# Norms finished in token layout and turned by plain transposes, instead of float32 matmuls with a diagonal matrix

## The chip, the cores and the metric

The kernel runs on one core of a Trainium2 chip, written in Bass with the Tile framework, which fixes the order of each engine's instructions before the run. The metric is the device time in microseconds of one execution; a kernel is timed in several runs, and the median counts. The engines are TensorE (PE), VectorE (DVE), ScalarE (ACT), GpSimd (POOL) and SyncE (SP, which issues the loads).

## What is computed

Two transformer blocks on S = 256 tokens with D = 1024 features, all in float32. The first has two layers, the second two more:

```python
def rms_norm(x, g):
    y = xf * lax.rsqrt(jnp.mean(xf * xf, axis=-1, keepdims=True) + EPS)
    return (y * g.astype(f32)).astype(x.dtype)
def layer_norm(x, g, b):
    mu = jnp.mean(xf, -1, keepdims=True)
    var = jnp.mean(jnp.square(xf - mu), -1, keepdims=True)
    return ((xf - mu) * lax.rsqrt(var + LN_EPS) * g + b).astype(x.dtype)

def even_layer(x, ...):  z = rms_norm(x, g_norm) @ w_in; ...; return x + y @ w_out   # two attentions
def odd_layer(x, ...):   z = rms_norm(x, g_norm) @ w_in; ...; return x + (y * silu(g)) @ w_out   # retention
def first_block(x, ...): return rms_norm(odd_layer(even_layer(x)), final_norm)

def second_block(x, ...):
    h = layer_norm(x, ln_in_g, ln_in_b)
    for l in range(DEPTH):               # DEPTH = 2
        m = hybrid_mixer(h, ...)
        h = layer_norm(ALPHA * h + m, ln1_g[l], ln1_b[l])
        f = swiglu(h, ...) if l % 2 == 0 else moe_swiglu(h, ...)   # dense, then 8 experts, top 2
        h = layer_norm(ALPHA * h + f, ln2_g[l], ln2_b[l])
    return h
```

## The kernel before

**Layout.** The activations x stay in SBUF as [128 tokens, 2 tiles, 1024 features]. Products with weights need them turned, features on partitions. So each norm writes `xT[0]` and `xT[1]`, [128 features, 8 chunks, 256 tokens]: two float32r parts (high and low) whose sum is the float32 value. The weights stream from HBM as raw float32 into `w_raw`, in units of 128 x 2048. ACT copies each into its high part `w_hi` (L56), DVE subtracts for the low part `w_lo` (L58). A float32 product is then three matmuls, hi x hi, hi x lo and lo x hi (`mm3`, L177 to L179).

**Order around a norm.** `out_units` computes the last matrix product ahead of a norm. Its last four weight units go tile by tile of the tokens: first all matmuls of tile 0 (48, with 512 columns, into two PSUM banks), then the 48 of tile 1. As soon as tile 0 is emitted, `done(0, acc[0])` emits its norm, then come the matmuls of tile 1; the scheduler places the instructions of both on each engine. The norm of tile 1 is kept in `self.late` and emitted by `finish`, after the next `token_units` has emitted the matmuls of tile 0 for its three units (24 each, 256 columns); those of tile 1 follow. Ahead of the experts it is the 16 small matmuls of the router that stand in place of the three units. Two tiles each for the norms at the start, behind the even layer (RMS norms), behind the odd layer, mixer 0, the feed-forward and mixer 1 (layer norms) make twelve tile norms. A last layer norm behind the experts goes to the output and is not turned.

**One norm of a tile.** On DVE: for a layer norm x * ALPHA + acc (L344) and the statistics (L345, L347), (x - mean) * g (L356), and the factor r = 1/sqrt(var) by Newton steps on 128x1 values (`rsqrt`, L286 to L296). Then `diagonal` (L372) makes a 128x128 matrix with r on its diagonal. `transpose` multiplies each 128x128 chunk of x by it on PE as a float32 matmul (L386; the trace shows each as two passes), which turns and scales at once. For a layer norm, the shift b is added in the same bank by a bfloat16 matmul first (L382), from a table of three-part shifts that the start loads and splits. From PSUM, ACT copies the high parts and DVE subtracts the low ones (L406; L394 and L398 where RMS scales are applied). x itself gets r * x + b only later (L364), in `rows_later` three units on, or in the experts spread over ACT and POOL.

Of the kernel before, what the change touches and what calls it, by code (L numbers as in the profile page):

```python
# [15 lines left out]
ALU = mybir.AluOpType  # L16
# [8 lines left out]
class Weights:  # L25
    """The weights in the order of their use: loaded and split into two float32r parts ahead of it."""
# [48 lines left out]
class Side:  # L75
    """Work in stages that goes between the weight units. A stage that yields "pre" has its next one before a unit."""
# [39 lines left out]
class Stack:  # L116
    def __init__(self, nc, tc, ctx, a, out, order, dbg=None):
# [11 lines left out]
        self.pend, self.late, self.update, self.todump = [], None, [], None  # L129
# [7 lines left out]
    def spare(self):  # L137
        """A buffer [128, 2, 1024] among those of the weights."""
        return self.wpools[0].tile([128, 2048], F32, name="w_raw")[:].rearrange("p (t d) -> p t d", t=2)

    def rows(self, *aps, queue=None):
        """One or two rows of 1024, on all partitions."""
        t = self.spare()
        for i, ap in enumerate(aps):
            if ap is None:
                continue
            (queue or self.nc.gpsimd).dma_start(t[:, i, :], bass.AP(tensor=ap.tensor, offset=ap.offset,  # L147
                                                                  ap=[[0, 128], [1, D]]))
        return [t[:, i, :] for i in range(len(aps))]

    def load_shifts(self):
        for g in range(2):
            for j in range(3):
                p = 64 * g + 8 * j
                self.nc.gpsimd.dma_start(self.xs[p:p + 8, 1, 0:256].rearrange("p (i f) -> p i f", i=2),
                                         self.a["shifts"][2 * g:2 * g + 2].rearrange("i c f -> c i f"))

    def split_shifts(self):
        """The shifts of the norms, [(part, chunk), 128 features] in three bfloat16 parts that add up to them."""
        v = self.nc.vector  # L160
        for g in range(2):
            r = slice(64 * g, 64 * g + 24)
            t, f = self.shifts[r].rearrange("p i f -> p (i f)"), self.xs[r, 1, 0:256]
            v.tensor_copy(self.chunk[r], self.pick[r, 0:8])
            for j in range(2):
                v.tensor_copy(t, f)
                v.scalar_tensor_tensor(f, t, self.pick[r, 8 + j:9 + j], f, op0=ALU.mult, op1=ALU.add)
            v.tensor_copy(t, f)

    def shift(self, i):  # L170
        r = slice(64 * (i // 2), 64 * (i // 2) + 24)
        return self.shifts[r, i % 2], self.chunk[r]

# [7 lines left out]
    def evac(self):  # L181
        """What is left to do with the products of the units before; some of it a unit later."""
# [8 lines left out]
    def feature_unit(self, done, chunks=2):  # L191
        """[features, tokens] of a unit's columns."""
# [10 lines left out]
    def token_units(self, *dones):  # L203
        """[tokens, features] of the columns of some units, tile by tile of the tokens."""
# [24 lines left out]
    def rows_later(self):  # L229
        for _ in range(3):  # L230
            yield
        self.normalise()

    def normalise(self, spread=False):
        for f in self.update:
            f(spread)
        self.update = []
        self.dump(self.todump, True)
# [42 lines left out]
    def rsqrt(self, mul, eps, *var):  # L281
        """1 / sqrt(var * mul + eps) of each, by Newton's steps from a guess on the bits; the guess is negative."""
# [27 lines left out]
    def squares(self, tt, acc):  # L310
        """The sums of the squares of a tile of x, by halves of the features; acc has its banks for the squares."""
# [5 lines left out]
    def rms(self, g, accs, between=0):  # L317
        """xT gets the parts of the normalised tiles of x; g has the scales of the features."""
        ds = []
        for tt, acc in accs:  # L320
            ss, ms = self.squares(tt, acc), self.small(1, "ms")
            self.nc.vector.tensor_add(ms[:], ss[:, 0:1], ss[:, 1:2])
            r, = self.rsqrt(1.0 / D, 1e-6, ms[:])
            ds.append(self.diagonal(r))
# [3 lines left out]
        for (tt, _), r in zip(accs, ds):  # L328
            ins = self.transpose(tt, self.x[:, tt], r, scale=g)
        return ins  # L330

    def layer_norm(self, tt, g, b, bT=None, acc=None, rms=None):
        """Of ALPHA * x + acc; or of the normalised x by the scales in rms, with their norm's factor in this one's."""
# [21 lines left out]
        for d in self.halves():  # L355
            v.scalar_tensor_tensor(xs[:, d], y[:, d], mv[:, 0:1], g[:, d], op0=ALU.subtract, op1=ALU.mult)  # L356

        def update(spread=False):
            for d in self.halves():
                if spread:  # L360
                    self.nc.scalar.activation(xs[:, d], xs[:, d], AF.Copy, scale=r)
                    self.nc.gpsimd.tensor_add(xs[:, d], xs[:, d], b[:, d])
                else:
                    v.scalar_tensor_tensor(xs[:, d], xs[:, d], r, b[:, d], op0=ALU.mult, op1=ALU.add)  # L364
        if bT is None:
            return update()
        self.update.append(update)
        return self.transpose(tt, xs, self.diagonal(r), bT)

    def diagonal(self, r):  # L370
        dr = self.sm.tile([128, 128], F32, name="dr", bufs=2)
        self.last = self.nc.vector.tensor_scalar(dr[:], self.ident, r, None, op0=ALU.mult)  # L372
        return dr

    def transpose(self, tt, src, dr, shift=None, scale=None):
        """The two parts of src * r * scale + shift go to xT; dr has the scales r of the tokens on its diagonal."""
        t = slice(tt * 128, (tt + 1) * 128)
        for n in range(2):
            ps = self.bank([128, 4, 128])
            if shift is not None:  # L380
                rows, chunk = shift
                self.nc.tensor.matmul(ps[:], rows, chunk[:, 4 * n:4 * n + 4, None].to_broadcast([24, 4, 128]),  # L382
                                      start=True, stop=False, skip_group_check=True)
            for k in range(4):
                d = slice((4 * n + k) * 128, (4 * n + k + 1) * 128)
                self.nc.tensor.matmul(ps[:, k, :], src[:, d], dr[:], start=shift is None, stop=True,  # L386
                                      skip_group_check=True)
# [14 lines left out]
    def split_into(self, hi, lo, src, scale=1.0):  # L402
        """The two float32r parts of src * scale; scale is a power of two."""
# [5 lines left out]
    def dump(self, name, now=False):  # L409
        if self.late and not now:  # L410
            self.todump = name
        elif name in self.dbg:
            self.nc.gpsimd.dma_start(self.dbg[name].rearrange("(t p) d -> p t d", p=128), self.x[:])

# [37 lines left out]
    def transpose_p(self, P, P1, P0):  # L452
        """[keys, head, (queries 0 on keys 0, queries 1 on keys 0, queries 1 on keys 1)]."""
# [10 lines left out]
    def pv(self, o, PT, v0, v1, start, stop):  # L464
        """o [(head, d), tokens] += v^T P^T; v0, v1: [128 keys, 2 heads, 64]."""
# [8 lines left out]
    def setup(self, dm):  # L474
# [3 lines left out]
        cst = c.tile([128, 210], F32, name="cst")  # L478
# [13 lines left out]
        self.pick = cst[:, 200:210]  # L492
        self.identr, self.cm = (c.tile([128, 128], F32R, name=n) for n in ("identr", "cm"))
        self.xT = [c.tile([128, 8, S], F32R, name=f"xT{i}") for i in range(2)]
        self.chunk = c.tile([128, 8], BF, name="chunk")
        self.shifts = c.tile([128, 2, 128], BF, name="shifts")
        self.load_shifts()
        accs = [(tt, [self.bank([128, 512]) for _ in range(2)]) for tt in range(2)]
        self.W.after = self.rms(self.scales[:, 0], accs, 1)
        self.W.after_act = self.acted  # L500

# [1 line left out]
    def even(self):  # L503
        nc, a, tc = self.nc, self.a, self.tc
        with ExitStack() as ctx:
# [17 lines left out]
            def masks():  # L523
                yield
                yield
                with self.W.behind(self.W.after), self.W.behind(self.W.after_act):
# [4 lines left out]
                    self.split_shifts()  # L531
# [95 lines left out]

            def done(tt, acc):
                self.add_to_x(tt, acc, 1.0)
                return self.rms(self.scales[:, 1], [(tt, acc)])  # L630
            self.out_units(list(range(0, 8)), part, acc, done)
        self.dump("d0")

# [1 line left out]
    def odd(self):  # L635
        nc, a, tc, v = self.nc, self.a, self.tc, self.nc.vector
        with ExitStack() as ctx:
# [88 lines left out]
            bT = self.shift(0)  # L726
# [4 lines left out]
            def done(tt, acc):  # L731
                self.add_to_x(tt, acc, 1.0)
                return self.layer_norm(tt, gi, bi, bT, acc, rms=(gf, scaled))
            self.out_units(list(range(8, 16)), part, acc, done)
        self.dump("d2")

# [1 line left out]
    def mixer(self, l):  # L738
        nc, a, tc, v, s = self.nc, self.a, self.tc, self.nc.vector, self.nc.scalar
        with ExitStack() as ctx:  # L740
# [91 lines left out]
            with tc.tile_pool(name="cmp", bufs=1) as cp:  # L832
# [141 lines left out]
                for j in range(2):  # L974
# [4 lines left out]
                    if j == 0:  # L979
                        g, b = self.rows(a["ln1_g_2"][l], a["ln1_b_2"][l])  # L980
                        bT = self.shift(1 + l)
# [8 lines left out]
            self.out_units([4, 5, 6, 7, 0, 1, 2, 3], part, done=lambda tt, acc: self.layer_norm(tt, g, b, bT, acc),  # L990
                           ahead=2 - l)
        self.dump(f"d{3 + 2 * l}")

# [1 line left out]
    def ffn(self):  # L995
        nc, a, tc, v = self.nc, self.a, self.tc, self.nc.vector
        with ExitStack() as ctx:
# [26 lines left out]
            bT = self.shift(3)  # L1024
# [408 lines left out]
```

## Time and profile before

| what | value |
| --- | --- |
| median of three runs | 1434.82 us (1432.43 to 1436.96) |
| span of the profiled execution | 1432.7 us |
| PE busy | 1393.4 us (97%) |
| DVE busy | 1097.8 us (77%) |
| ACT busy | 828.4 us (58%) |
| POOL busy | 99.5 us (7%) |
| float32 passes with the diagonal (L386) | 192, 28.2 us busy, 13.5 us idle ahead of them |

The profile shows one execution, and its time is its span. Busy times are those of the whole span; the stages differ, and a line's idle time is that of its engine just ahead of the line's instructions, with what ended most of it. A matmul's duration in a row is longer than its step: it overlaps the next, so costs are taken from the distance between starts.

### The profile page before, as it was taken

Reading aid. Unit: us, or ns where it says so; the run is one execution under the profiler, and the core shown is the slowest. Engines: PE = TensorE matmul, PEld = TensorE weight load, DVE = VectorE, ACT = ScalarE, POOL = GpSimd, SP = SyncE. Lnnn points to the kernel's source line nnn. Section 1 sums busy time; section 2 is a strip of 40 time slices with the busy share of each in tenths; the row PEclk is TensorE's granted clock in tenths of the full one; section 3 lists DMA queues with packets and bytes.
Section 4 is the critical chain, followed back from the end, with each engine's and each line's share of the span. In section 5 each row is a group of like instructions: output and inputs, shape, how many; then the busy total and the mean of one; then the engine's idle time right before and its main releaser. Section 6 shows DMA issues by size and latency. Waiting matters only on the chain. (4 is left out here: it accounts for less than half of the span.)

```text
span 1432.7 us, 25068 instructions
## 1 busy us (share of the span) xinstructions
PE 1393.4 (97%) x10075; PEld 1289.3 (90%) x10075; DVE 1097.8 (77%) x1816; ACT 828.4 (58%) x1388; POOL 99.5 (7%) x136
## 2 busy tenths in 40 slices
PE   7999999999999999999999999998999999999995
PEld 7999999789999789989999889987999999999983
DVE  7766656567777679878655388777989989989987
ACT  7665555454455347544444247645777777777762
POOL 1000000000000100010000000003010110120110
PEclk9999999999999999999999999998999999999997
DMA  7633343336444466326455446322989889889882
GB/s 292 233 147 138 129 148 138 134 138 226 155 175 155 132 232 224 118 67 264 178 184 199 176 145 253 118 98 83 361 332 339 314 327 346 307 335 355 309 329 85
DMA packets 45435, 301.50 MB, mean 210 GB/s; under 512 B 6000, under 2 KB 6368, under 8 KB 10624
## 3 DMA queue, kind: packets, MB, share of 16 engines
q1 hardware_dynamic: 42336, 293.40, 55.4%
q0 software_dynamic: 2832, 6.42, 1.7%
q8 instruction: 81, 1.33, 0.4%
q14 instruction: 42, 0.34, 0.1%
q10 hardware_dynamic: 144, 0.01, 0.0%
HBM read 298.73 MB, written 1.05 MB: 209 GB/s over the span
## 5 line engine op out<-in xcount | busy, mean ns | idle before, releaser
L58 DVE TENSOR_TENSOR w_lo<-w_raw,w_hi 128x1024 fp32r<-128x1024 f32 x553 | 673.5, 1249 | 170.0 <-ACT w_hi L56 169.7
L56 ACT ACTIVATE w_hi<-w_raw 128x1024 fp32r<-128x1024 f32 x553 | 560.9, 1056 | 212.2 <-PE ps L179 103.4
L177 PE MATMUL ps<-xT,w_hi 128*128 128x256 f32 x1096 | 310.6, 283 | 0.0
L178 PE MATMUL ps<-xT,w_hi 128*128 128x256 f32 x1096 | 308.0, 281 | 0.0
L179 PE MATMUL ps<-xT,w_lo 128*128 128x256 f32 x1096 | 307.8, 281 | 0.0
L177 PEld LDWEIGHTS ps<-xT,w_hi 128*128 128x128 f32 x1096 | 206.4, 188 | 1.7 <-issue 1.5
L178 PEld LDWEIGHTS ps<-xT,w_hi 128*128 128x128 f32 x1096 | 206.6, 188 | 0.0
L179 PEld LDWEIGHTS ps<-xT,w_lo 128*128 128x128 f32 x1096 | 206.5, 188 | 0.0
L178 PE MATMUL ps<-w_lo,xe 128*128 128x256 f32 x704 | 199.3, 283 | 1.3 <-DVE w_lo L58 1.1
L177 PE MATMUL ps<-w_hi,xe 128*128 128x256 f32 x704 | 198.9, 283 | 0.0
L179 PE MATMUL ps<-w_hi,xe 128*128 128x256 f32 x704 | 198.8, 282 | 0.0
L177 PE MATMUL ps<-w_hi,xT 128*128 128x256 f32 x528 | 148.7, 282 | 0.0
L178 PE MATMUL ps<-w_lo,xT 128*128 128x256 f32 x528 | 147.8, 280 | 0.0
L179 PE MATMUL ps<-w_hi,xT 128*128 128x256 f32 x528 | 146.9, 280 | 0.1
L178 PEld LDWEIGHTS ps<-w_lo,xe 128*128 128x128 f32 x704 | 132.5, 188 | 3.0 <-DVE w_lo L58 2.2
L177 PEld LDWEIGHTS ps<-w_hi,xe 128*128 128x128 f32 x704 | 132.9, 189 | 0.6
L179 PEld LDWEIGHTS ps<-w_hi,xe 128*128 128x128 f32 x704 | 132.6, 188 | 0.0
L177 PEld LDWEIGHTS ps<-w_hi,xT 128*128 128x128 f32 x528 | 100.0, 189 | 0.3
L178 PEld LDWEIGHTS ps<-w_lo,xT 128*128 128x128 f32 x528 | 100.0, 189 | 0.3
L179 PEld LDWEIGHTS ps<-w_hi,xT 128*128 128x128 f32 x528 | 99.2, 189 | 0.4 <-DVE xT L398 0.3
L441 ACT ACTIVATE P<-ps,sm_mx 128x128 f32<-128x128 f32 (+1 forms) x128 | 52.1, 419 | 37.3 <-DVE sm_mx L435 37.3
L1214 POOL TENSOR_TENSOR x<-x,part 128x512 f32<-128x512 f32 x28 | 47.5, 1724 | 337.2 <-ACT part L1210 274.8
(365 smaller groups left out, 2219.9 us busy)
## 6 DMA issues: line engine op xcount, KB each, us to landing
w_raw<-in_wts SPq DMA_DIRECT2D x271, 1024.0 KB, 4.9
w_raw<-in_wth SPq DMA_DIRECT2D x11, 512.0 KB, 4.5
w_raw<-in_ln_g POOLq DMA_DIRECT2D x3, 512.0 KB, 4.2
w_raw<-in_ln_b POOLq DMA_DIRECT2D x3, 512.0 KB, 5.1
x<-in_x SPq DMA_DIRECT2D x4, 256.0 KB, 3.5
out<-x SPq DMA_DIRECT2D x4, 256.0 KB, 2.1
dec<-in_dec POOLq DMA_DIRECT2D x1, 512.0 KB, 9.7
w_raw<-in_final_norm POOLq DMA_DIRECT2D x1, 512.0 KB, 3.8
```

What stands on the lines that cost most here:

```text
L56: self.nc.scalar.activation(hi[:, d], t[:, d], AF.Copy)
L58: self.nc.vector.tensor_sub(lo[:, d], t[:, d], hi[:, d].bitcast(F32))
L177: t.matmul(out, l[0], r[0], start=start, stop=False, skip_group_check=True)
L178: t.matmul(out, l[0], r[1], start=False, stop=False, skip_group_check=True)
L179: t.matmul(out, l[1], r[0], start=False, stop=stop, skip_group_check=True)
L441: s.activation(p[:, h, :], src[:, h, :], AF.Exp, bias=mx[:, o + h:o + h + 1], accum_out=rs[:, o + h:o + h + 1])
L1214: nc.gpsimd.tensor_add(x, x, t[:])
```

## The change

A norm is finished on DVE and then only turned. For a layer norm, DVE computes x = x * r + b in two halves of the features, directly after r, and PE turns the eight 128x128 chunks by plain transposes with the identity (L336 in the changed kernel). For an RMS norm, DVE writes xn = x * r to a spare weight buffer (in two halves too), and xn is turned. The diagonal matrices, the shift matmuls, the shifts' loads and their splitting, and the later update of x go, as do hooks for debugging output and docstrings.

```diff
-    def rms(self, g, accs, between=0):
+    def rms(self, g, accs, xn, between=0):
         for tt, acc in accs:
             ...
             r, = self.rsqrt(1.0 / D, 1e-6, ms[:])
-            ds.append(self.diagonal(r))
+            for d in self.halves():
+                self.last = v.tensor_scalar(xn[:, tt, d], self.x[:, tt, d], r, None, op0=ALU.mult)
         ...
-        for (tt, _), r in zip(accs, ds):
-            ins = self.transpose(tt, self.x[:, tt], r, scale=g)
+        for tt, _ in accs:
+            ins = self.transpose(tt, xn[:, tt], scale=g)

-    def layer_norm(self, tt, g, b, bT=None, acc=None, rms=None):
+    def layer_norm(self, tt, g, b, acc=None, rms=None, last=False):
         ...
         for d in self.halves():
             v.scalar_tensor_tensor(xs[:, d], y[:, d], mv[:, 0:1], g[:, d], op0=ALU.subtract, op1=ALU.mult)
-        def update(spread=False):
-            ...
-        self.update.append(update)
-        return self.transpose(tt, xs, self.diagonal(r), bT)
+        for d in self.halves():
+            self.last = v.scalar_tensor_tensor(xs[:, d], xs[:, d], r, b[:, d], op0=ALU.mult, op1=ALU.add)
+        if not last:
+            return self.transpose(tt, xs)

-    def transpose(self, tt, src, dr, shift=None, scale=None):
+    def transpose(self, tt, src, scale=None):
         for n in range(2):
             ps = self.bank([128, 4, 128])
-            if shift is not None:
-                rows, chunk = shift
-                self.nc.tensor.matmul(ps[:], rows, chunk[:, 4 * n:4 * n + 4, None].to_broadcast([24, 4, 128]),
-                                      start=True, stop=False, skip_group_check=True)
             for k in range(4):
                 d = slice((4 * n + k) * 128, (4 * n + k + 1) * 128)
-                self.nc.tensor.matmul(ps[:, k, :], src[:, d], dr[:], start=shift is None, stop=True,
-                                      skip_group_check=True)
+                self.nc.tensor.transpose(ps[:, k, :], src[:, d], self.ident)
...
-                self.pend.append(self.rows_later())
...
+            xn = self.spare()
+            nc.gpsimd.memset(xn[:, :, 0:1], 0.0)
...
-            self.normalise(True)
```

The scheduler gives the norms another place in PE's queue. The following is PE's order of before in mixer 0, at the norm of tile 0, where ps_7053 and ps_7054 are the two banks of tile 1 and dr_7140 is the diagonal of tile 0; 18 more matmuls of tile 1 stand ahead of these rows, behind the last one of tile 0.

```order
L177 MATMUL ps_7053<-w_hi_6900,yc0_5618 128x512
L178 MATMUL ps_7053<-w_lo_6901,yc0_5618 128x512
L179 MATMUL ps_7053<-w_hi_6900,yc1_5619 128x512
L177 MATMUL ps_7054<-w_hi_6900,yc0_5618 128x512
L386 MATMUL ps_7142<-dr_7140,x_107 128x128 [waits DVE_49]
L386 MATMUL ps_7142<-dr_7140,x_107 128x128 x3
L386 MATMUL ps_7150<-dr_7140,x_107 128x128 x4
L178 MATMUL ps_7054<-w_lo_6901,yc0_5618 128x512
L179 MATMUL ps_7054<-w_hi_6900,yc1_5619 128x512
```

In the changed kernel this is PE's order at the norm of tile 0, where ps_7026 is the second bank of tile 0, ps_7027 and ps_7028 are those of tile 1, and L154 to L156 are the three matmuls of a product.

```order
L154 MATMUL ps_7026<-w_hi_7037,q0_5600 128x512
L155 MATMUL ps_7026<-w_lo_7038,q0_5600 128x512
L156 MATMUL ps_7026<-w_hi_7037,q1_5601 128x512
L336 MATMUL ps_7116<-cst_109,x_107 128x128 [waits DVE_49]
L336 MATMUL ps_7116<-cst_109,x_107 128x128 x3
L336 MATMUL ps_7123<-cst_109,x_107 128x128 [waits DVE_49]
L336 MATMUL ps_7123<-cst_109,x_107 128x128 x3
L154 MATMUL ps_7027<-w_hi_6766,yc0_5598 128x512
L155 MATMUL ps_7027<-w_lo_6767,yc0_5598 128x512
```

The norm's PE instructions moved from behind 22 matmuls of tile 1 to ahead of all 48. Mixer 1 has the same two orders; at the other norms the transposes stand within a few matmuls of the place that the float32 matmuls had.

On DVE, the same place of before reads so, where rs_y is the factor r and L406 writes the low part of xT:

```order
L296 SCALAR_TENSOR_TENSOR rs_y_7127<-rs_t_7128,rs_y_7127 128x1 [waits DVE_49]
L372 TENSOR_SCALAR dr_7140<-cst_109,rs_y_7127 128x128 [waits DVE_49]
L364 SCALAR_TENSOR_TENSOR x_107<-x_107,rs_y_7127,w_raw_6636 128x512 [waits DMASW3_49,PE_49]
L406 TENSOR_TENSOR xT1_127<-ps_7142,xT0_126 128x4x128 [waits Activation_49]
L364 SCALAR_TENSOR_TENSOR x_107<-x_107,rs_y_7127,w_raw_6636 128x512 [waits PE_49]
L406 TENSOR_TENSOR xT1_127<-ps_7150,xT0_126 128x4x128 [waits Activation_49]
L58 TENSOR_TENSOR w_lo_7159<-w_raw_6676,w_hi_7158 128x1024 [waits DMAHW4_49]
```

And so in the changed kernel, where L325 is x = x * r + b and L355 writes the low part of xT:

```order
L261 SCALAR_TENSOR_TENSOR rs_y_7101<-rs_t_7102,rs_y_7101 128x1 [waits DVE_49]
L325 SCALAR_TENSOR_TENSOR x_107<-x_107,rs_y_7101,w_raw_6610 128x512 [waits DMASW5_49,DVE_49]
L325 SCALAR_TENSOR_TENSOR x_107<-x_107,rs_y_7101,w_raw_6610 128x512
L355 TENSOR_TENSOR xT1_127<-ps_7116,xT0_126 128x4x128 [waits Activation_49]
L355 TENSOR_TENSOR xT1_127<-ps_7123,xT0_126 128x4x128 [waits Activation_49]
L58 TENSOR_TENSOR w_lo_7131<-w_raw_6650,w_hi_7130 128x1024 [waits DMAHW4_49,Activation_49]
```

The update of x no longer waits for PE but stands ahead of it, and the diagonal is gone.

## Rows read from the trace of the kernel before

**Rows 1.** The page: span of the profiled execution.

```profile
span 1432.7 us, 25068 instructions
```

**Rows 2.** Windows: start:end, length, busy time of PE, PEld, DVE, ACT, POOL; clock, DMA share, GB/s.

```profile
36.00:320.00 284.00, 283.47 (x2092) 257.34 (x2091) 178.94 (x311) 157.78 (x355) 9.15 (x18) 1.00 0.42 151
...
1100.00:1400.00 300.00, 298.17 (x2104) 278.16 (x2103) 274.83 (x302) 225.33 (x296) 41.27 (x24) 1.00 0.87 329
```

**Rows 3.** Groups by line and shape: busy us, mean ns; idle us before, its releasers.

```profile
L386 PE MATMUL ps<-dr,x 128*128 128x128 f32 x192 | 28.2, 306 | 13.5 <-DVE dr L372 13.5
...
L364 DVE SCALAR_TENSOR_TENSOR x<-x,rs_y,w_raw 128x512 f32<-128x512 f32 x16 | 11.8, 751 | 9.1 <-PE ps L386 8.5 <-DMA w_raw<-in_ln_b 0.3
```

**Rows 4.** Timeline of PE, its three waits: start us, us, instruction [idle before].

```profile
8.44 5.23 PE L386 MATMUL ps<-dr,x 128*128 128x128 f32 x32 [8.44 <-DVE dr L372]
...
518.56 2.51 PE L386 MATMUL ps<-dr,x 128*128 128x128 f32 x16 [2.10 <-DVE dr L372]
520.72 0.56 PE L177 MATMUL ps<-w_hi,xT 128*128 128x256 f32 x1
...
979.92 3.79 PE L386 MATMUL ps<-dr,x 128*128 128x128 f32 x16 [2.99 <-DVE dr L372]
983.35 0.36 PE L1093 MATMUL ps<-routerp,xT 128*128 128x16 f32 x1
```

**Rows 5.** Timeline of PE, odd layer, first tile's norm.

```profile
493.37 0.40 PE L179 MATMUL ps<-w_hi,y 128*128 128x512 f32 x1
...
494.23 0.50 PE L177 MATMUL ps<-w_hi,y 128*128 128x512 f32 x1
...
499.95 0.39 PE L177 MATMUL ps<-w_hi,y 128*128 128x512 f32 x1
500.19 0.40 PE L178 MATMUL ps<-w_lo,y 128*128 128x512 f32 x1
500.42 1.95 PE L386 MATMUL ps<-dr,x 128*128 128x128 f32 x16
502.12 0.48 PE L179 MATMUL ps<-w_hi,y 128*128 128x512 f32 x1
```

**Rows 6.** Timeline of PE in the experts, eleven plain transposes of activations.

```profile
1030.78 0.28 PE L179 MATMUL ps<-w_hi,xe 128*128 128x256 f32 x1
1030.91 1.36 PE L1174 MATMUL ps<-cst,he 128*128 128x128 f32 x11
1032.03 0.37 PE L177 MATMUL ps<-w_hi,xe 128*128 128x256 f32 x1
```

**Rows 7.** Timeline of DVE: start, odd layer, mixer 0, mixer 1.

```profile
11.33 2.36 DVE L58 TENSOR_TENSOR w_lo<-w_raw,w_hi 128x1024 fp32r<-128x1024 f32 x2 [1.40 <-ACT w_hi L56]
...
503.07 1.28 DVE L406 TENSOR_TENSOR xT<-ps,xT 128x512 fp32r<-128x512 f32 x2
...
637.99 0.29 DVE L372 TENSOR_SCALAR dr<-cst,rs_y 128x128 f32<-128x128 f32 x1
...
966.24 0.29 DVE L372 TENSOR_SCALAR dr<-cst,rs_y 128x128 f32<-128x128 f32 x1
```

**Rows 8.** Timeline of PE: the mixers, first tile's norm.

```profile
633.12 0.39 PE L177 MATMUL ps<-w_hi,yc 128*128 128x512 f32 x1
...
638.33 2.05 PE L386 MATMUL ps<-dr,x 128*128 128x128 f32 x16
...
646.31 0.28 PE L177 MATMUL ps<-w_hi,xT 128*128 128x256 f32 x1
...
961.36 0.40 PE L177 MATMUL ps<-w_hi,yc 128*128 128x512 f32 x1
```

**Rows 9.** Windows of half a microsecond: odd layer, experts' start (columns of rows 2).

```profile
520.00:520.50 0.50, 0.50 (x5) 0.50 (x4) 0.50 (x2) 0.35 (x1) 0.00 (x0) 0.50 1.00 426
...
523.00:523.50 0.50, 0.50 (x4) 0.50 (x4) 0.50 (x1) 0.00 (x0) 0.00 (x0) 0.60 0.97 246
...
984.00:984.50 0.50, 0.50 (x5) 0.50 (x5) 0.13 (x1) 0.50 (x2) 0.50 (x1) 0.80 0.00 0
```

More of the change, by code (lines that the diff above doesn't have):

```diff
@@ L149, in rows @@
         return [t[:, i, :] for i in range(len(aps))]
[L151 to L172, printed above, removed]
     def mm3(self, out, l, r, start, stop):
@@ L225, in finish @@
             if ahead:
-                self.pend.append(self.rows_later())
                 self.W.ahead()
[L229 to L238, printed above, removed]
     def out_units(self, chunks, parts, acc=None, done=None, last=4, ahead=2):
@@ L356, in layer_norm @@
             v.scalar_tensor_tensor(xs[:, d], y[:, d], mv[:, 0:1], g[:, d], op0=ALU.subtract, op1=ALU.mult)
-        def update(spread=False):
[L359 to L366, printed above, removed]
-        self.update.append(update)
-        return self.transpose(tt, xs, self.diagonal(r), bT)
[L370 to L373, printed above, removed]
-    def transpose(self, tt, src, dr, shift=None, scale=None):
+        for d in self.halves():
[3 more added lines that the diff above has]
+    def transpose(self, tt, src, scale=None):
         t = slice(tt * 128, (tt + 1) * 128)
@@ L407, in split_into @@
         return self.nc.vector.scalar_tensor_tensor(lo, src, scale, hi.bitcast(F32), op0=ALU.mult, op1=ALU.subtract)
[L409 to L413, printed above, removed]
     def scores(self, q, kz, extra):
@@ L477, in setup @@
         self.xs = self.spare()
-        cst = c.tile([128, 210], F32, name="cst")
+        cst = c.tile([128, 200], F32, name="cst")
         self.scales = c.tile([128, 2, 8], F32, name="scales")
@@ L491, in setup @@
         self.cma, self.cmm = (cst[:, i:i + 32].rearrange("p (t n) -> p t n", t=2) for i in (136, 168))
-        self.pick = cst[:, 200:210]
         self.identr, self.cm = (c.tile([128, 128], F32R, name=n) for n in ("identr", "cm"))
         self.xT = [c.tile([128, 8, S], F32R, name=f"xT{i}") for i in range(2)]
-        self.chunk = c.tile([128, 8], BF, name="chunk")
-        self.shifts = c.tile([128, 2, 128], BF, name="shifts")
-        self.load_shifts()
         accs = [(tt, [self.bank([128, 512]) for _ in range(2)]) for tt in range(2)]
-        self.W.after = self.rms(self.scales[:, 0], accs, 1)
+        self.W.after = self.rms(self.scales[:, 0], accs, self.xs, 1)
         self.W.after_act = self.acted
@@ L1023, in ffn @@
             g, b = self.rows(a["ln2_g_2"][0], a["ln2_b_2"][0])
-            bT = self.shift(3)
             part = lambda c: [t[:, c, :] for t in h]
-            self.out_units(list(range(22)), part, done=lambda tt, acc: self.layer_norm(tt, g, b, bT, acc))
-        self.dump("d4")
+            self.out_units(list(range(22)), part, done=lambda tt, acc: self.layer_norm(tt, g, b, acc))
     def moe(self):
@@ L1254, in moe @@
             for tt in range(2):
-                self.layer_norm(tt, g, b)
+                self.layer_norm(tt, g, b, last=True)
                 for d in self.halves():
@@ L1374, in constants @@
         np.eye(128), bm, np.where(seen, 0.0, NEG), seen)], axis=1).astype(np.float32)
-    j = np.arange(24)[:, None]
-    c["pick"] = np.concatenate([j % 8 == np.arange(8), -(j >= 8 * np.arange(1, 3)).astype(np.float32)], axis=1)
-    c["cst"] = np.concatenate([c["cst"], np.pad(np.pad(c.pop("pick"), ((0, 40), (0, 0))), ((0, 64), (0, 0)), mode="wrap")], axis=1).astype(np.float32)
     c["iota"] = np.broadcast_to(np.arange(S, dtype=np.float32), (128, S)).copy()
```

19 lines of the change are left out of this document (6 added, 13 removed).

## The prediction

> **What bounds the kernel now.** I read the page first: the profiled execution spans 1432.7 us [rows 1]. The median of the three runs is 1434.82 us, 2.1 us more, and they spread over 4.5 us; I work out a difference against the span and add it to the median. Then the busy time by windows: TensorE (PE) is busy 283.47 of 284 us in one long stretch and 298.17 of 300 in the experts, where VectorE (DVE) with 274.83 is close behind [rows 2]. So PE sets the pace, and a microsecond of PE work that goes is a microsecond of time wherever PE does not wait instead. Where it waits is told by the list of groups: the float32 passes of the old norm (L386) carry 13.5 us of idle time, all of it put down to the diagonal that DVE makes (L372) [rows 3]. That is three waits: 8.44 us at the start, 2.10 at the second tile of the odd layer, 2.99 at that of the second mixer [rows 4]. At the other eight of the twelve tile norms PE has work while the norm's chain runs on DVE. The question is therefore for each place: is the norm on PE's path as work, as a wait, or hidden, and does the change alter which?
>
> **What a tile's norm costs on PE.** Old: 16 passes stand between L178 at 500.19 and L179 at 502.12; less one step of a matmul (0.24, from 499.95 to 500.19) that is 1.69 us, 0.106 each. The two shift matmuls take 494.23 - 493.37 - 0.24 = 0.62 [rows 5]. New: eight plain transposes. The nearest row is the 11 of L1174, the same operation in the same shape: 1032.03 - 1030.78, less 0.12 for a matmul of half the columns (half of 0.24), is 1.13, or 0.103 each, 0.82 for eight [rows 6]. So a tile of a layer norm saves 1.69 + 0.62 - 0.82 = 1.5 us of PE work, a tile of an RMS norm 0.87. The rows say that a float32 transpose takes one pass where a float32 matmul takes two. The Trainium skill, "TensorE: Matmul & The Clock Gate", section "Terms", has transpose mode as four times faster for float32; by that the eight would take 16 x 0.106 / 4, an estimate of 0.42, and the ten norms behind the start would gain 4 us more. The row of L1174 does not bear this out, and it decides.
>
> **What the new chain costs on DVE.** Old: behind the factor r comes the 128x128 diagonal (0.29 us [rows 7]), and x * r + b (L364, 0.751 us a half [rows 3]) waits until PE is done with x. New: x * r + b stands ahead of the transposes; four of them wait for each half. The first half is ready 0.75 us after r, 0.46 later than the diagonal was, the second 0.75 after it. The DVE work itself is the same; in a layer norm the diagonal goes.
>
> **Both mixers, first tile.** Here the order matters. Before, 22 of the second tile's 48 matmuls run while DVE works out the norm, from 633.12 on; the passes follow at 638.33 and the rest until 646.31, in all 13.19 us [rows 8]. In the changed order the eight transposes stand directly behind the first tile's last matmul and ahead of all 48. PE takes its instructions in order, so from 633.12 it waits for the chain, and nothing else of its queue can pass. The chain does not start earlier: r is there at 637.99, the first half at 638.74, the second at 639.49 [rows 3, 7], and the last transpose ends at 639.9. The 48 matmuls take 13.19 - 1.69 = 11.5 at full speed: 651.4.
>
> Then the clock. In the odd layer 2.1 us of idle time were followed by a granted clock of 0.50 (1.2 GHz) from 520.0 to 523.4 (0.60 as the mean of its last half microsecond), so 3.4 us of work at half speed, which lose half of it, 1.7. At the experts' start the clock was at 0.50 when work began again at 979.92 and came back at 984.2: 4.3 us, 2.1 lost [rows 4, 9]. An idle stretch of 5.6 us should cost as much; I take 1.8, between the two (bounds 1.5 and 2.1). So the second tile ends at 653.2, 6.9 later. Against this stand the two shift matmuls, which lay ahead of the first tile's end and go: -0.6. First tile: **+6.3**, with bounds of 6.0 and 6.6.
>
> Mixer 1 repeats it: the second tile began at 961.36 and the diagonal at 966.24 [rows 7, 8], so the first half would be there at 966.99, 5.6 us after PE ran out. Also +6.3.
>
> **Both mixers, second tile.** It lies behind three units of matmuls as before, and the stall in front has given DVE and ScalarE time, not taken it. In mixer 0 nothing waited there, so the full 1.5 comes off. In mixer 1 PE waited 2.99 for the diagonal and went on at half speed until 983.35 [rows 4]. Now the first half is there 0.46 after the moment at which the passes began, the second at 981.1; four transposes at half speed (0.21 each) take it to 982.0: -1.3, less 0.1 for a wait. I take -1.5 and -1.2; the bounds are 0 (the chain, longer by the scaling, becomes visible) and -1.5.
>
> **Even layer, odd layer, feed-forward.** In these the transposes still stand among the second tile's matmuls, so the first tile's norm stays hidden as a wait. Even: the first tile gains 0.87; in the second, two scalings by r replace the diagonal, and I count half: **-1.3** (bounds -0.9 and -1.7). Odd: the second tile is set by DVE, whose queue runs through splits of weights behind the first tile's evacuations (L406 at 503.07 [rows 7]). These can start about 1.0 earlier, as the transposes end near 501.8, so the second tile's factor comes about 1.0 earlier, but 0.75 for the first half and 0.75 for the second follow, then four transposes. The row shows passes from 518.56 and the next matmul at 520.72 [rows 4]; the new one comes at about 519.6: **-1.1** (bounds 0 and -2). The first tile's saving only lengthens PE's wait. Feed-forward: first tile -1.5, second between 0 and -1.5, where I take -0.3, since the chain reaches further and the last matmul ahead comes earlier: **-1.8**.
>
> **Start.** PE does 32 passes from 8.44 to 13.67 [rows 4], and DVE then idles 1.40 before the first weight split at 11.33 [rows 7]. The four scalings are not in the trace; between a 128x128 one (0.29) and the two-tensor form of full width (0.751 [rows 3]) I take 0.5. They stand where the second diagonal stood, at 11.33 - 1.40 - 0.29 = 9.64, and end at 11.64, so the split comes 0.3 later. Transposes begin 1.7 later than the passes did, but are 16 and not 32. The slower clock at the start then reaches further into the first unit, 0.5. **+0.8**, with bounds of 0 and +2.2. The loads and twelve small DVE operations of the shifts, which go, stood beside a busy PE: 0, as do the updates of x that leave ScalarE and GpSimd in the experts.
>
> **The sum.** 0.8 - 1.3 - 1.1 - 1.8 + (6.3 - 1.5) + (6.3 - 1.2) = +6.5 us. On the span that is 1439.2, on the median 1441.3; I say 1441.
>
> **Rivals.**
> *Only the cheaper PE work counts (faster).* If the two first tiles of the mixers did not stall, the ten norms behind the start would give up to 8 x 1.5 + 2 x 0.87 = 13.7 us, and the time would be 1421. For it: PE is the bound and the work is on it. Against it: the two rows of order show eight transposes that wait for DVE ahead of 48 matmuls that wait for nothing. To be faster by 0.3% the two stalls must be 10.8 us smaller together than I have them, almost all of their 11.2 us of idle time. Chance 0.07.
> *The stalls are there, but the others give them back.* If the clock costs 1.5 in each mixer and every other norm gives what its bound allows (even -1.7, odd -2, feed-forward -3.0, the mixers' second tiles -3.0, start 0), the sum is 2 x 6.0 - 9.7 = +2.3, time 1437; half way to it is the edge of a difference that can be told. For it: the terms of those places are cut by guesses. Against it: at the odd layer and at mixer 1 the trace shows the wait for DVE. Chance 0.33.
> *The transposes do not help to raise the clock.* Then the low stretch counts from the first matmul behind them: the eight transposes take 0.82 more in each mixer and the sixteen at the start 1.65 more, 3.3 together, time 1444. In the trace 11 transposes among matmuls at full clock leave it full [rows 6]; none stands behind an idle stretch, so nothing here excludes it. The Trainium skill, the same page, "Part 4: PE-mode transpose", says that in transpose mode the full clock does not engage; no run here shows that. Chance 0.18.
>
> **How the numbers follow.** The forecast itself has 0.42. Three runs that spread over 4.5 us can tell a change of about 0.3%, 4.3 us, from none. Slower by more: the forecast and the third rival, 0.60. Within: the second, 0.33. Faster: the first, 0.07. The range leaves the first rival out, takes the low bounds of all terms with the runs' spread (1434.5) and the high ones with the clock rival (1446.5).
>
> **What would show it.** In the mixers' first tiles, PE idle for about 5.6 us ahead of the transposes, twice, with DVE named, and the clock at 0.50 behind it; 48 matmuls without a norm between them. Second tiles: eight transposes of about 0.1 us with no shifts. At the odd layer a wait for DVE of about 3 us ahead of the second tile. At the start, the first matmul near 14 us. The prediction is wrong if the mixers' stalls are much shorter than 5 us, or if the transposes take 0.05 or 0.2.

## The result: 1.1% slower, and where the time lies

The changed kernel takes 1451.92 us (median of 4 runs, 1450.66 to 1452.3), before 1435.29: a ratio of 1.0114, 95% interval 1.0101 to 1.0126. The forecast of 1441 had the sign, but less than half of the size. The profiled execution spans 1450.4 us, 17.7 more than before.

The page of the changed kernel, against [rows 1]: the busy time of PE hardly moved, though 96 float32 matmuls with a diagonal and 16 shift matmuls became 96 transposes.

```profile
span 1450.4 us, 24819 instructions
PE 1393.5 (96%) x9963; PEld 1291.6 (89%) x9963; DVE 1095.8 (76%) x1804; ACT 826.7 (57%) x1384; POOL 89.8 (6%) x127
```

PE's waits in the changed kernel (what waited for what: us in total, times, longest). Before, the norms' waits were 13.5 us [rows 3]; now they are 30.1, of which 10.9 are the start.

```profile
PE ps L336 <- DVE x L325: 19.2, 5, 5.5
PE ps L336 <- DVE w_raw L290: 10.9, 1, 10.9
```

The timeline of PE in the changed kernel at the mixers' first tiles answers to [rows 8]. The second tile's first matmul now stands behind the wait: PE runs out at 636.57 and has its first transpose at 642.09, 5.52 us later; at mixer 1 the wait is 5.51.

```profile
636.17 0.40 PE L156 MATMUL ps<-w_hi,q 128*128 128x512 f32 x1
642.09 1.97 PE L336 MATMUL ps<-cst,x 128*128 128x128 f32 x8 [5.52 <-DVE x L325]
643.71 0.78 PE L154 MATMUL ps<-w_hi,yc 128*128 128x512 f32 x1
...
970.21 0.40 PE L156 MATMUL ps<-w_hi,q 128*128 128x512 f32 x1
976.12 1.97 PE L336 MATMUL ps<-cst,x 128*128 128x128 f32 x8 [5.51 <-DVE x L325]
```

Windows of the changed kernel there (columns of rows 2; the last but two is the clock). The clock is at half when the transposes start and is back within the second window: about 4.1 us of work at half speed, 2.1 lost.

```profile
642.00:642.50 0.50, 0.41 (x2) 0.42 (x3) 0.50 (x2) 0.00 (x0) 0.00 (x0) 0.50 0.00 0
...
646.00:646.50 0.50, 0.50 (x3) 0.45 (x2) 0.00 (x0) 0.00 (x0) 0.00 (x0) 0.85 0.00 0
```

The two stalls are as forecast, and do not make 17.7 us. To find the rest I set the start of the same matmul of a weight product in both traces side by side, all along. The changed kernel falls behind where no norm is at all: by 2.2 us from 54 to 246 us, 2.5 from 327 to 469 us, 1.3 from 681 to 770 us. There PE does nothing but matmuls that the change doesn't touch. These are the same two matmuls of the feed-forward, 600 apart, first in the kernel before and then in the changed one: 71.0 us, then 72.0. The step went from 0.1183 to 0.1200 us.

```profile
684.58 0.28 PE L179 MATMUL ps<-xT,w_lo 128*128 128x256 f32 x1
...
755.58 0.28 PE L179 MATMUL ps<-xT,w_lo 128*128 128x256 f32 x1
```

```profile
693.67 0.28 PE L156 MATMUL ps<-xT,w_lo 128*128 128x256 f32 x1
...
765.67 0.28 PE L156 MATMUL ps<-xT,w_lo 128*128 128x256 f32 x1
```

Some 4,900 matmuls of 256 columns read xT (3 x 1096 of feature units, 3 x 528 of token units, whose mean step went from 0.1167 to 0.1199). In a feature unit the weights are the operand that is loaded and xT the one that streams through, in a token unit it is the other way round. With 1.7 ns and 3.2 ns more each they account for 5.6 + 5.1 = 10.7 us at most; the mean over all feature-unit matmuls rose by 1.5 ns, which makes it about 10. Matmuls of other operands (y, h, xe) kept their step.

### The profile page after: what moved, and what is told of

Same layout as the page of the kernel before. It is cut to its first block, busy times and chain, and to the rows that moved or that the text cites. A ratio compares the mean times of both kernels' runs of the same rounds, so it can differ in the third digit from the quotient of the medians.

```text
span 1450.4 us, 24819 instructions
## 1 busy us (share of the span) xinstructions
PE 1393.5 (96%) x9963; PEld 1291.6 (89%) x9963; DVE 1095.8 (76%) x1804; ACT 826.7 (57%) x1384; POOL 89.8 (6%) x127
## 5 line engine op out<-in xcount | busy, mean ns | idle before, releaser
L154 PE MATMUL ps<-xT,w_hi 128*128 128x256 f32 x1096 | 312.6, 285 | 0.0
L156 PE MATMUL ps<-xT,w_lo 128*128 128x256 f32 x1096 | 309.7, 283 | 0.0
L154 PEld LDWEIGHTS ps<-xT,w_hi 128*128 128x128 f32 x1096 | 210.1, 192 | 1.7 <-issue 1.5
L155 PEld LDWEIGHTS ps<-xT,w_hi 128*128 128x128 f32 x1096 | 210.0, 192 | 0.0
L156 PEld LDWEIGHTS ps<-xT,w_lo 128*128 128x128 f32 x1096 | 209.9, 192 | 0.0
L154 PE MATMUL ps<-w_hi,xe 128*128 128x256 f32 x704 | 199.1, 283 | 0.0
L156 PE MATMUL ps<-w_hi,xe 128*128 128x256 f32 x704 | 198.8, 282 | 0.0
L154 PE MATMUL ps<-w_hi,xT 128*128 128x256 f32 x528 | 150.7, 286 | 0.3 <-ACT xT L353 0.2
L156 PE MATMUL ps<-w_hi,xT 128*128 128x256 f32 x528 | 148.4, 284 | 0.1
L154 PEld LDWEIGHTS ps<-w_hi,xe 128*128 128x128 f32 x704 | 133.0, 189 | 0.6
L156 PEld LDWEIGHTS ps<-w_hi,xe 128*128 128x128 f32 x704 | 132.8, 189 | 0.0
L154 PEld LDWEIGHTS ps<-w_hi,xT 128*128 128x128 f32 x528 | 102.0, 193 | 1.4 <-ACT xT L353 0.8
L156 PEld LDWEIGHTS ps<-w_hi,xT 128*128 128x128 f32 x528 | 101.0, 192 | 0.3 <-DVE xT L347 0.3
L155 PE MATMUL ps<-w_lo,hT 128*128 128x512 f32 x176 | 69.4, 395 | 0.0
```

Of the source, the lines that this page charges most:

```text
L154: t.matmul(out, l[0], r[0], start=start, stop=False, skip_group_check=True)
L155: t.matmul(out, l[0], r[1], start=False, stop=False, skip_group_check=True)
L156: t.matmul(out, l[1], r[0], start=False, stop=stop, skip_group_check=True)
```

## The experiments

**Where the operands lie.** The tables of shifts were 544 bytes of each partition, allocated between xT and the weight buffers, and the constants shrank by 64 ahead of xT. Without the tables, w_hi's first buffer starts 57344 = 7 x 8192 bytes behind xT[0], before it was 57888. All buffers of weights and both xT are 8192 apart, so the distance of any of them from xT, modulo 8192, went from 544 to 0. The operands of a single matmul are slices of these buffers and lie a multiple of 512 bytes further apart or closer, so 544 and 32 are the same modulo 512, as are 576 and 64. The experiments change nothing but widths of allocations; each engine's order stays as it was. The edit for a distance of 32 (8 elements; 16 for 64 bytes, 32 for 128, 64 for 256, 144 for 576):

```diff
-        self.xT = [c.tile([128, 8, S], F32R, name=f"xT{i}") for i in range(2)]
+        wide = c.tile([128, 8 * S], F32R, name="xT0"), c.tile([128, 8 * S + 8], F32R, name="xT1")
+        self.xT = [t[:, :8 * S].rearrange("p (k s) -> p k s", k=8) for t in wide]
```

> The changed kernel, with every buffer behind xT moved up by 32 bytes: xT[1] is allocated 32 bytes wider. No instruction and no order changes. Before the change xT started at 32 modulo 64 bytes in its partition and the weights w_hi, w_lo at 0; after it both start at 32, since 608 bytes of shift tables and a part of the constants are gone. Here xT is at 32 and the weights at 0 again. Theory A (matmuls are slower by some 2% when the two operands start in the same half of 64 bytes): the step of a matmul on xT goes back from 0.120 to 0.117 us, and the time falls by 8 to 9 us, to 1443. Theory B (the step is slower for another reason, the engines' traffic in the new order): 1452, no change. Theory C (what counts is that the weights start at a multiple of 64, xT doesn't matter): 1443 as in A.

> The changed kernel with xT and every buffer behind it moved up by 32 bytes (a constant ahead of xT is allocated 32 bytes wider): xT and the weights both start at 0 modulo 64. No instruction and no order changes. Theory A (same half of 64 bytes is slow): 1452, no change. Theory B (layout has no part): 1452. Theory C (weights at a multiple of 64 are fast): 1443.

> The changed kernel with xT moved up by 32 bytes and the buffers behind it by 64: xT starts at 0 modulo 64, the weights at 32. No instruction and no order changes. Theory A (different halves of 64 bytes are fast): 1443. Theory B (layout has no part): 1452. Theory C (weights off a multiple of 64 are slow): 1452.

> The kernel before, with every buffer behind xT moved up by 32 bytes, so that xT and the weights both start at 32 modulo 64, as in the changed kernel. No instruction and no order changes, and the norms are the old ones. Theories A and C: the step of a matmul on xT rises from 0.117 to 0.120 us, and the time by 8 to 9 us, to 1444. Theory B (the slower step belongs to the new norms): 1435, no change.

In the second of these only the tile ahead of xT is wider, by 32 bytes; in the third both are:

```diff
-        self.identr, self.cm = (c.tile([128, 128], F32R, name=n) for n in ("identr", "cm"))
+        self.identr = c.tile([128, 128], F32R, name="identr")
+        self.cm = c.tile([128, 136], F32R, name="cm")[:, :128]
```

Measured: 1442.46, 1451.22 and 1441.33 us for the changed kernel, exactly as theory A said: theories B and C fall. But the kernel before, at 1424.86, became faster by 0.7% (0.9906 to 0.995) where A and C had it slower by 9 us. So A falls too: what the two operands have modulo 64 does not decide. The distances in the four runs are 32, 0, 32 and 576, and these order them. That made theory F, which the next runs test, on both kernels:

> The kernel before with its two tables of shifts allocated ahead of xT instead of behind it, so that xT moves up by 544 bytes and the weights stay where they are. No instruction and no order changes. The runs so far say: with w_hi[first buffer] - xT[0] counted modulo 8192 bytes (all buffers of weights and both xT are 8192 apart), the step of a 256-column matmul on xT is 0.120 us at a distance of 0 (the changed kernel, and its copy with both moved by 32), 0.117 and 0.118 at 32, 0.117 and 0.118 at 544 (the kernel before) and 0.117 and 0.115 at 576. Here the distance is 0. Theory F (the distance of the two operands sets the step, whatever the norms): steps of 0.120, and 8 to 10 us more than before, 1444. Theory B (something of the changed norms' traffic is needed as well): 1435.

> The changed kernel with xT[1] allocated 64 bytes wider: the weights lie at a distance of 64 modulo 8192. No instruction and no order changes. Theory F with a period of 512 bytes or less: as at 576, steps of 0.117 and 0.115, and 10 us less than at 32, 1432. Theory F with a longer period, or with the start modulo 64 in it as well: any step between 0.115 and 0.120, 1432 to 1451. Theory B: 1452.

> The changed kernel with xT[1] allocated 576 bytes wider: the weights lie at a distance of 576 modulo 8192, as in the fastest layout of the kernel before. No instruction and no order changes. Theory F: steps of 0.117 and 0.115, and the same 10 us below the 1442.5 of distance 32 that the kernel before shows between 544 and 576: 1432.5. The change itself would then cost in this layout what it costs at 32, 7 to 8 us over 1424.9. A rival theory, that the gain at 576 belongs to buffers that are placed otherwise in the two kernels (those of the layers, not xT and the weights): 1442.

The edit of the first of them only moves two lines, so that xT lies behind the tables:

```diff
+        self.chunk = c.tile([128, 8], BF, name="chunk")
+        self.shifts = c.tile([128, 2, 128], BF, name="shifts")
         self.xT = [c.tile([128, 8, S], F32R, name=f"xT{i}") for i in range(2)]
-        self.chunk = c.tile([128, 8], BF, name="chunk")
-        self.shifts = c.tile([128, 2, 128], BF, name="shifts")
```

Measured: the kernel before at distance 0 takes 1443.32 us, +0.52% (0.35 to 0.69%); the changed one 1430.43 at 64 and 1432.3 at 576. All as theory F said, with a period of 512 bytes or less. The same two matmuls as above, in the kernel before at distance 0 (72.0 us apart) and in the changed kernel at 64 (68.0):

```profile
690.95 0.28 PE L179 MATMUL ps<-xT,w_lo 128*128 128x256 f32 x1
...
762.95 0.28 PE L179 MATMUL ps<-xT,w_lo 128*128 128x256 f32 x1
```

```profile
684.33 0.28 PE L156 MATMUL ps<-xT,w_lo 128*128 128x256 f32 x1
...
752.33 0.28 PE L156 MATMUL ps<-xT,w_lo 128*128 128x256 f32 x1
```

All layouts, with the changed kernel's two last ones from below:

| distance of weights from xT, mod 8192 | 600 steps, us | step, us | old norms, us | changed norms, us | changed norms and order, us |
| --- | --- | --- | --- | --- | --- |
| 0 | 72.0 | 0.1200 | 1443.3 | 1451.9, 1451.2 | 1436.2 |
| 32 | 71.0 | 0.1183 | | 1442.5, 1441.3 | |
| 64 | 68.0 | 0.1133 | | 1430.4 | 1418.3 |
| 128 | 71.2 | 0.1187 | | | 1431.0 |
| 256 | 72.0 | 0.1200 | | | 1435.0 |
| 544 | 71.0 | 0.1183 | 1434.8 | | |
| 576 | 68.0 | 0.1133 | 1424.9 | 1432.3 | |

At equal distance the change costs 1451.9 - 1443.3 = 8.6 us (0), 1442.5 - 1434.8 = 7.7 (32 against 544, the same step; 6.5 by the second run at 32), 1432.3 - 1424.9 = 7.4 (576).

**The mixers' order.** The transposes of the first tile are emitted behind 24 of the second tile's matmuls and held there:

```diff
+                    if tt and callable(turn) and w is units[1][0]:
+                        with self.tc.issue_after(ins.ins):
+                            self.W.after = turn()
+                        self.W.split(self.W.used + ahead)
...
-                    self.W.after = done(0, acc[0])
-                    self.W.split(self.W.used + ahead)
+                    turn = done(0, acc[0])
+                    if not callable(turn):
+                        self.W.after = turn
+                        self.W.split(self.W.used + ahead)
...
+        if hold:
+            return lambda: self.transpose(tt, xs)
```

> The changed kernel, layout unchanged (distance 0), with the transposes of both mixers' first tiles emitted behind 24 of the second tile's 48 matmuls, and held there, in place of ahead of all 48; the next weight splits of VectorE are emitted behind them. Theory of the stall (PE waits 5.5 us for x * r + b in each mixer, and the clock at half speed costs about 2 more): both waits go, and with them 5.5 + 2.0 each, less at most 0.5 of new waits: 1452 - 14 to 15 = 1437 to 1438. Rival (the wait moves on: the later transposes make the next layer's first matmuls wait for xT, or the late splits make them wait for weights): 1443 to 1450.

Measured: 1436.22 us, 15.7 less, and level with the kernel before (1435.68 beside it). The timeline of PE in this kernel at the first mixer shows the transposes between two matmuls, with no wait:

```profile
643.11 0.39 PE L155 MATMUL ps<-w_lo,q 128*128 128x512 f32 x1
643.40 1.32 PE L345 MATMUL ps<-cst,x 128*128 128x128 f32 x8
644.48 0.48 PE L156 MATMUL ps<-w_hi,q 128*128 128x512 f32 x1
```

The rival, a wait that moves on, is not there: this kernel's waits for x * r + b in all are 9.1 us, 10.1 less than the 19.2, close to the 11.0 of the two stalls.

**Both together, and the distance carried on.**

> Both repairs together: the transposes of the mixers' first tiles behind 24 matmuls of the second tile, and xT[1] allocated 64 bytes wider, which puts the weights at a distance of 64 modulo 8192 from xT. If stall and step are independent, the sum holds: 1436.2 with the order alone, less the 20 us that the 64 bytes gave without it (1451.9 to 1431), 1416; it should beat the kernel before by 1.3%, and the kernel before in its own best layout (1424.9) by 8 to 9 us. Rival (the faster steps make DVE or the loads the bound, and part of the gain turns into waits): 1420 to 1426.

> As the kernel with both repairs, at a distance of 128. If the step goes on falling with the distance (0.120 at 0, 0.118 at 32, 0.1147 at 64 for the matmuls of feature units): 0.110 to 0.114, and 1406 to 1414. If the operands only must not fall together within 64 bytes: as at 64, 1416. If other operands then fall together: 1417 to 1436.

> As the kernel with both repairs, at a distance of 256. If the step goes on falling with the distance up to half of 512 bytes: under 1412. If it has a floor from 64 on: 1416. If it rises again: up to 1436.

Measured: 1418.27 us, ratio 0.9879 (0.986 to 0.9898), so stall and step add up to within 2.3 us (1416 expected; the rival began at 1420), and the version beats the kernel before in either layout. At 128 it is 1431.04, at 256 1434.95: the step does not go on falling, nor stay; 64 is a good place and 256 as bad as 0. That the operands only must not fall together within 64 bytes is thereby wrong.

The last run moves the experts' tokens xe by 64 bytes too, by a wider buffer ahead of them:

```diff
-                c = [io.tile([128, 8, 8], F32, name=f"r_c{j}", bufs=1) for j in range(2)]
+                c = [io.tile([128, 64 + 16 * j], F32, name=f"r_c{j}", bufs=1)[:, :64].rearrange("p (a b) -> p a b", a=8) for j in range(2)]
```

> As the kernel with both repairs, at a distance of 64, and in the experts' stage a small buffer allocated 64 bytes wider, which moves the gathered tokens xe (read with the weights by 2112 matmuls of 256 columns, at 0.119 us a step in all runs so far) by 64 bytes against the weights. If the distance counts there too and gets better: 0.115 to 0.117 and up to 8 us less, 1408 to 1415, as far as PE still sets the pace beside DVE and the loads. If it gets worse: 0.120, 1417 to 1419. If these matmuls are set by something else: 1416.

Measured: 1412.64 us, ratio 0.9843 (0.9827 to 0.986), 5.6 less than without; the mean step of the matmuls on xe went from 0.1190 to 0.1176, which is 2.9 us over 2112 of them. The wider buffer moved the experts' hT by 64 bytes against the weights as well. It is read by 528 matmuls of 512 columns, and their mean step went from 0.2329 to 0.2292: another 2.0 us. These are the same two of them, 60 apart, in the kernel with both repairs (14.00 us) and in this one (13.74):

```profile
1123.11 0.39 PE L154 MATMUL ps<-w_hi,hT 128*128 128x512 f32 x1
...
1137.11 0.39 PE L154 MATMUL ps<-w_hi,hT 128*128 128x512 f32 x1
```

```profile
1121.43 0.40 PE L154 MATMUL ps<-w_hi,hT 128*128 128x512 f32 x1
...
1135.17 0.39 PE L154 MATMUL ps<-w_hi,hT 128*128 128x512 f32 x1
```

It is the fastest version, 1.6% under the kernel before.

## Why the prediction was wrong

**The step that failed** is one that put a price of nothing: "The loads and twelve small DVE operations of the shifts, which go, stood beside a busy PE: 0." As work they cost next to nothing. As space they did not: without their 544 bytes the weights lie at another distance from xT, and the step of some 4,900 matmuls was 1 to 3% longer. The prediction took the steps of matmuls from rows of before and held them fixed for everything that the diff does not touch. The kernel before shows the price by itself: the same tables on the other side of xT make it 7.6 us slower (1443.3 against 1435.7 beside it). Of the 16.6 us, 8 to 9 are this: what is left of them at equal distance is 8.6 or 7.7. The range did not follow from its own terms either: the high bounds add up to 2.2 - 0.9 - 1.5 + 2 x 6.6 = +13.0, so 1447.8, and 1451.1 with the clock rival, not 1446.5. Had it reached the measured 1451.9 in this way, it would have been luck, since no term of it is the step.

**The other half was the mechanism forecast.** With the step as before (run a_xT32_w0, distance 32) the change costs +0.54% (0.33 to 0.76%), 7.7 us, where the sum said +6.5. The starts of the same matmuls in the kernel before and in this run show the terms:

| between | before, us | run, us | difference | term | forecast |
| --- | --- | --- | --- | --- | --- |
| in the first unit | 16.68 | 16.67 | 0.0 | start 0.0 | +0.8 |
| ahead of the even norm | 286.40 | 285.75 | -0.65 | -0.65 | 0 |
| behind it | 326.89 | 325.05 | -1.84 | even -1.2 | -1.3 |
| ahead of the odd norm | 468.85 | 467.05 | -1.80 | 0.0 | 0 |
| behind it | 539.11 | 537.19 | -1.92 | odd -0.1 | -1.1 |
| ahead of mixer 0's norm | 611.24 | 609.39 | -1.85 | +0.1 | 0 |
| near the end of its tile 1 | 644.91 | 649.69 | +4.78 | first tile +6.6 | +6.3 |
| behind its tile 1's norm | 680.79 | 684.23 | +3.44 | second tile -1.3 | -1.5 |
| behind the feed-forward's norm | 906.43 | 908.47 | +2.04 | -1.4 | -1.8 |
| ahead of mixer 1's norm | 938.61 | 940.67 | +2.06 | 0.0 | 0 |
| at the end of its tile 1 | 971.04 | 979.38 | +8.34 | first tile +6.3 | +6.3 |
| in the first expert | 1016.66 | 1025.37 | +8.71 | second tile +0.4 | -1.2 |
| in the last experts | 1391.24 | 1399.37 | +8.13 | -0.6 | 0 |

The mixers' first tiles are right: order, wait and price. The even layer, the feed-forward and mixer 0's second tile are near their terms. The 0.65 us go between 42 and 53 us, in the even layer's attention, where PE waited 0.48 us for VectorE before and 0.15 us for ScalarE in this run. The twelve operations of the shifts had held VectorE from 24.2 to 28.2 us; that their going is the reason is not shown.

The table compares single executions, and two of its small terms do not hold in the next one. Run a_xT0_w32 has the same distance and the same order. There the start is +0.7 and the odd layer -1.5, both near the forecast, and the change costs 1441.33 - 1434.79 = 6.5 us; that it meets the forecast sum to a tenth is luck, as the other run's 7.7 shows. The matmul of the table's first row starts between 16.67 and 18.42 us in the changed kernel's six layouts.

At the odd layer's second tile the wait is 3.74 us in a_xT32_w0 where 2.10 stood before [rows 4]; I had foreseen about 3, but not that the clock would fall while PE still waited. This is the timeline and the clock of a_xT32_w0 there:

```profile
516.38 1.94 PE L336 MATMUL ps<-cst,x 128*128 128x128 f32 x8 [3.74 <-DVE x L325]
518.16 0.58 PE L154 MATMUL ps<-w_hi,xT 128*128 128x256 f32 x1
```

```profile
516.00:516.50 0.50, 0.12 (x1) 0.14 (x2) 0.50 (x2) 0.00 (x0) 0.00 (x0) 0.50 0.89 377
...
522.00:522.50 0.50, 0.50 (x5) 0.50 (x5) 0.00 (x0) 0.00 (x0) 0.00 (x0) 0.73 0.00 0
```

PE works at half speed from 516.38 to about 522.3, 5.9 us, where before it was 3.4 [rows 9]: 1.25 us more are lost, and the term goes from -1.1 to about 0. In a_xT0_w32 the wait is as long, but the clock is back at about 520.0, after 2.9 us of work:

```profile
517.08 1.94 PE L336 MATMUL ps<-cst,x 128*128 128x128 f32 x8 [3.67 <-DVE x L325]
```

```profile
519.50:520.00 0.50, 0.50 (x4) 0.50 (x4) 0.34 (x2) 0.15 (x1) 0.00 (x0) 0.54 0.64 262
```

So the odd layer's forecast lies between two executions whose stretches at half speed differ by 3.0 us, or 1.5 lost.

One term was mis-sized in both: mixer 1's second tile, +0.4 and +0.2 against -1.2. At the experts' start the changed kernel has its transposes at 996.07 and the next router matmul 1.80 later; before, the passes took 3.43 [rows 4]. But the wait ahead of them grew from 2.99 us [rows 4] to 3.83. And the clock, which before was back at 984.2 [rows 9] and at half again from about 987.6 to 994.4, stayed at half in the changed kernel until near 1011.4. First the kernel before, then the changed one:

```profile
987.50:988.00 0.50, 0.00 (x0) 0.00 (x0) 0.43 (x4) 0.00 (x0) 0.00 (x0) 0.61 0.62 131
...
994.00:994.50 0.50, 0.50 (x5) 0.50 (x4) 0.02 (x1) 0.38 (x1) 0.50 (x1) 0.56 0.00 0
```

```profile
996.00:997.00 1.00, 0.94 (x5) 0.94 (x6) 0.93 (x5) 0.00 (x0) 0.00 (x0) 0.50 0.00 0
...
1011.00:1012.00 1.00, 1.00 (x8) 1.00 (x8) 0.42 (x1) 0.59 (x3) 1.00 (x1) 0.81 0.00 0
```

From the first pass or transpose to the first expert's matmul (996.64 before, 1013.00 in the changed kernel) that is 11.1 us at half speed before and 15.3 in the changed kernel. So the saved PE work was paid back in the wait and in the speed of the router and gather matmuls. In a_d64 and a_d576, where it was 12.7 and 12.5 us, the term is -0.7. That the shorter work caused the late return was not tried by itself.

**The rivals.** That only cheaper PE work counts is refuted for this order and half true with the other: at a distance of 0 the kernel with the order repaired beats the old norms by 1443.3 - 1436.2 = 7.1 us, at 64 against 576 by 1424.9 - 1418.3 = 6.6, where 13.7 were the most that the work could give. The kernel with the order repaired still waits 9.1 us for x * r + b and 11.4 us at the start, 7.0 more than the 13.5 before [rows 3], which is about the rest. That the others give the stalls back did not come: the change costs 7.7 and 6.5 us at a distance of 32, not 2.3. That transposes do not help to raise the clock is not shown: in the mixers it was back 4.1 us after they began, as after 4.3 us of float32 passes and router before [rows 4, 9], so the mixers do not bear out the rival. At the experts' start the clock did stay low, but other small matmuls stand there too. So the runs neither bear out nor exclude the rule of the Trainium skill, "TensorE: Matmul & The Clock Gate", "Part 4: PE-mode transpose". As for the price of a transpose, in the changed kernel's even layer eight of them begin at 315.61 and the next matmul at 316.67, 0.13 each with the gaps at both ends. Nothing shows of the factor of four that the Trainium skill has in "Terms" of the same page.

```profile
315.61 1.03 PE L336 MATMUL ps<-cst,w_raw 128*128 128x128 f32 x8
316.67 0.39 PE L154 MATMUL ps<-w_hi,xT 128*128 128x256 f32 x1
```

## What to carry to other kernels

A change that frees or moves buffers has a second effect on the layout; before its time is credited to its work, compare the step of matmuls that it does not touch, and measure both kernels at equal distances of their operands. A scheduler that places instructions anew can turn a hidden chain into a stall: look for an instruction that waits ahead of many that don't. A term of about a microsecond is not judged by one execution: here the start and the clock moved such terms by more than that. Here 64 bytes in one allocation were worth 21 us, more than the two stalls.

## What the runs showed of the hardware

The step of a 256-column float32r matmul with its own weights load depends on where its two operands lie relative to each other in a partition. On xT in 600 feature-unit matmuls of the feed-forward it is 0.1133 us at distances of 64 and 576 bytes (modulo 8192), 0.1183 at 32 and 544, 0.1187 at 128, 0.1200 at 0 and 256 (means over all feature units: 0.1146 to 0.1148, 0.1183, 0.1187, 0.1198). In the token units, where the operands change roles, 32 and 544 are the best: 0.1167 to 0.1170, then 0.1173 to 0.1177 at 64 and 576, 0.1189 at 128 and 0.1199 at 0 and 256. The experts' xe, in the role that xT has in the token units, agrees: 0.1190 at a distance of 128 modulo 512, in all runs but the last, and 0.1176 at 64. A pair of distances 512 apart gives the same step in the feed-forward, and it does not matter whether xT starts at 0 or 32 modulo 64 (1451.9 and 1451.2 at distance 0, 1442.5 and 1441.3 at 32).

Accesses of other engines are not the cause. Over the feature-unit steps during which VectorE, ScalarE and GpSimd all stood still the mean is 0.1200 at 0 (222 steps), 0.1181 at 32 (201) and 0.1152 at 64 (159). In the token units, with the DMA queues idle as well, it is 0.1199 at 0 (35 steps) and 0.1171 at 32 (30).

The mean duration of a weights load moved with the step only in part: 192 ns at 0 and 256, but 188 ns at 32, 64 and 128. The groups of the weights loads show this, in the changed kernel and at 64:

```profile
L154 PEld LDWEIGHTS ps<-xT,w_hi 128*128 128x128 f32 x1096 | 210.1, 192 | 1.7 <-issue 1.5
```

```profile
L154 PEld LDWEIGHTS ps<-xT,w_hi 128*128 128x128 f32 x1096 | 206.5, 188 | 1.7 <-issue 1.5
```

Which reads meet, and where, is open: no run separates the stream of one operand from the load of the other. Other distances than these seven were not tried, and the matmuls of 512 columns had their distance changed in the last run only, those on hT from 128 to 64 modulo 512: from 0.2329 to 0.2292 us.
